# A hybrid decoder step on one core: score products over 128 rows, 1 - beta from ScalarE, and the mixer's stores on another queue

## The chip, the core and the metric

The kernel runs on one core of a Trainium2 chip. The core has TensorE (PE, matrix products; PEld is its weight load), VectorE (DVE), ScalarE (ACT), GpSimd (POOL), and SyncE (SP), which here only issues DMA. ACT can issue DMA too, on a queue of its own. Products are written to PSUM; everything else lives in SBUF or in DRAM. The metric is the time of one execution in microseconds, the median over runs.

## The reference

One inference step of two layers over 1024 prompt tokens and 8 samples of 8 new tokens each, width 1024, all in float32. Layer 0 is stick-breaking attention (16 heads of 64), layer 1 an RWKV-7 mixer (16 heads with a 64 x 64 state); each is followed by a squared-ReLU MLP of width 4096, and each of the four sub-layers has an adaptive RMS norm before it. For attention,

```
z = q.k / 8 + bias[head]
log_beta = log_sigmoid(z);  log_1mb = where(mask, log_beta - z, 0)     # log(1 - beta)
tail = reverse_cumsum(log_1mb) - log_1mb
a = where(mask, exp(log_beta + tail), 0);   o = a @ v
```

so each weight is beta times the product of (1 - beta) over all later keys. The prompt attends to itself; the samples attend to 2048 cached keys in pages of 128 and to their own. The mixer mixes each token with the one before it, makes r, k, v by dense products and the decay, rate and gate by low-rank ones, and runs a recurrence over the tokens:

```
S = S * w_t - (S @ kk_t) b_t^T + v_t k_t^T;   y_t = S @ r_t
```

## The kernel before

**Foreground and background.** The tokens go in two halves: A has 576 prompt tokens, B has 448 prompt tokens and the 64 sample tokens. Tiles have 128 features as rows and tokens as columns. Dense layers (`dense`, lines 328 to 341) are the foreground: each weight tile is split into a high part (`wh`, ACT, L321) and a low part (`wl`, POOL L323 and DVE L324), and each output tile takes three products for each of its feature tiles (L337 to L339) on 288 or 512 columns. After each such triple `step` is called; it advances generators: `self.work`, the background, by `rate` steps per 512 columns, and `self.side`, work that stands beside a stage. The background is attention of A, attention of B, attention of the samples, then for each half `rw_units` (the mixer's preparation) and `rw_chains` (the recurrence by chunks of 64 tokens). So the order in which Python traces instructions weaves both together. The tile framework then orders each engine's instructions by a simulated time line of its own (`schedule_with_timeline_sim=True`); on the chip each engine runs its list in that order.

**Stages.** qkv of A, qkv of B with attention A behind it, output projection and MLP of A with attention B and the samples behind them, `mixer_in` of A, output projection and MLP of B with the mixer of A behind them, `mixer_in` of B, then the rest.

**Scores.** `att_stacks` loads q, k and v of a pair of heads and makes for each head `qh`, the high part of q in both halves of the 128 rows, `kk`, the high part of k in its own 64 rows and the low part in the others, and `ql`, the low part of q in 64 rows. `att_prompt` makes a score tile z of 128 queries by up to 512 keys with two products: L552, `qh` against `kk` over 128 rows, and L554, `ql` against `kk` over 64 rows. Tiles of 64 queries take both heads at once with plain products (L550). `stick` turns z into weights: beta by a sigmoid on ACT (L509), a mask on POOL on the diagonal (L560, L562), 1 - beta on POOL (L512), the carry into the last column (L514, L516), a running product from the right on DVE (L518), and the weights (L519). The weights are transposed on PE (L126), copied by ACT (L576) and multiplied with v (L585). The samples use the same `stick` with tiles of 256 keys.

**Mixer.** `mixer_in` runs three dense products through `dense_to`, which copies each output tile out of PSUM, half the time by ACT and half by DVE (`copy`), and stores it (L963). Beside them stand `lora_rates` and `lora_gate`, which load the normed input again (L889) and mix it (`xmix`: ACT L814, DVE L817) for small products; `xsplit`, the same for the next dense product; and `rw_gate`, which loads a weight (L944, L945), multiplies and stores (L952). `rw_value` transposes v and stores it for the chunks (L981). In the background `rw_unit` prepares two heads: it loads k and r, runs a chain over all engines, and stores seven kinds of pieces (L1070, L1090, L1119, L1120, L1133 to L1135). After every three (A) or four (B) units `rw_lanes` inverts their 32 x 32 blocks by 31 steps of forward substitution on DVE (L1161, L1163), two steps of it for every step of a unit. All these loads and stores are issued by SP, in one list with the weight loads (L318), which ACT issues only while the samples are attended to.

Of the kernel before, what the change touches and what calls it, by code (L numbers as in the profile page):

```python
# [20 lines left out]
NT = 8  # L21
# [34 lines left out]
SLOT = 576  # L56
# [3 lines left out]
C_H16, C_SELN, C_MQ = 1056, 1072, 1200  # L60
C_N = 1264


def make_consts():
# [22 lines left out]
    c[:, C_MQ:C_MQ + 64] = t < s  # L87
    c[p % 32 == 0, C_SELN:C_SELN + 64] = 1.0
# [4 lines left out]
class Kern:  # L93
# [361 lines left out]
    def att_setup(self, lp):  # L455
# [9 lines left out]
        for hd, r in enumerate(self.R2):  # L465
            nc.vector.tensor_copy(self.bias_2[r, :], self.bias[r, hd::2])
        self.pt = lp.tile([1, 8 * PAGES], I32, name="pt")
# [6 lines left out]
    def att_stacks(self, m, pt, sp):  # L474

# [13 lines left out]
        ql = sp.tile([128, SLOT], F32R, tag="ql", name="ql")[:, :pt.NP]  # L489
        for hd in range(2):  # L490
# [10 lines left out]
        return q, k, qs, ql, ks, v  # L501

    def stick(self, z, w, bias, bp, tag, carry, mask):
# [4 lines left out]
        p = bp.tile([128, W + 1], F32, tag=tag + "p", name="prod", bufs=4 if tag == "p" else 3)  # L508
        nc.scalar.activation(beta[:, :w], z, AF.Sigmoid, bias=bias, scale=0.125)  # L509
        if mask:  # L510
            mask(beta)
        nc.gpsimd.tensor_scalar(p[:, :w], beta[:, :w], -1.0, 1.0, ALU.mult, ALU.add)  # L512
# [9 lines left out]
    def att_prompt(self, m, pt, sp, bp, ps):  # L522

        nc = self.nc
        q, k, qs, ql, ks, v = self.att_stacks(m, pt, sp)
# [7 lines left out]
        for c, end in sorted(tiles, key=lambda t: t[1] - t[0]):  # L533
# [7 lines left out]
            for j, (e0, e1) in enumerate(pieces):  # L541
# [3 lines left out]
                for x, hs in enumerate(heads):  # L545
                    z = ps.tile([128, 512], F32, tag="z", name="z")
                    for hd in hs:
                        a = self.R2[hd]
                        if both:
                            nc.tensor.matmul(z[a, :w], q[a, qc], k[a, e0:e1], start=True, stop=True)  # L550
                            continue
                        nc.tensor.matmul(z[:, :w], qs[hd][:, qc], ks[hd][:, e0:e1], start=True,  # L552
                                         stop=False)
                        nc.tensor.matmul(z[:, :w], ql[a, qc], ks[hd][a, e0:e1], start=False,  # L554
                                         stop=True)

                    def mask(beta, w=w):
                        d = beta[:, w - n:w]
                        if both:
                            nc.gpsimd.tensor_mul(d, d, self.cst[:, C_MQ:C_MQ + 64])  # L560
                        else:
                            nc.gpsimd.affine_select(out=d, in_=d, compare_op=ALU.is_gt, fill=0.0,  # L562
                                                    base=0, pattern=[[-1, 128]],
                                                    channel_multiplier=1)
                    bias = self.bias_2[:, m:m + 1] if both else \
                        self.bias[:, 2 * m + x:2 * m + x + 1]
                    al, carry[x] = self.stick(z[:, :w], w, bias, bp, "p", carry[x],
# [47 lines left out]
    def att_sample(self, sp, bp, ps):  # L615
# [38 lines left out]
        def new_keys(b, qbd):  # L654
# [7 lines left out]
            def mask(beta):  # L662
                nc.gpsimd.tensor_mul(beta[:, :8], beta[:, :8], self.cst[:, C_MN:C_MN + 8])
            al, carry = self.stick(z[:, :8], 8, self.bias_s, bp, "s", None, mask)
# [18 lines left out]
        for n, (b, j) in enumerate(steps):  # L683
# [6 lines left out]
            al, carry = self.stick(z[:, :256], 256, self.bias_s, bp, "s", carry, None)  # L690
# [194 lines left out]
    def lora_mixed(self, ns, f, pt, c0, n, tmp):  # L885
# [846 lines left out]
```

## Time and profile before

| | us |
|---|---|
| median of three runs (lowest, highest) | 3774.43 (3769.27, 3775.43) |
| the profiled execution: time, span | 3787.43, 3785.7 |
| PE, DVE, ACT, POOL busy in the span | 3562.3, 2331.9, 1467.7, 1351.5 |
| mean granted clock of TensorE | 0.959 |

The profile is that of one execution. A row of a group gives line, engine, operation, output and inputs by the program's names, shapes and count, then busy time in us and the mean duration of one in ns, then the engine's idle time just ahead of these instructions and what ended it. A row of waits names the waiting instruction, what it waited for, us in total, times, and the longest in us. In a list in order of time the first column is the start in us and the second the duration. Ends of products are modelled, so durations of neighbours overlap and the distance between starts says what a product costs. "SPq" and "ACTq" are the sequencers that issue DMA.

### The profile page before, as it was taken

To read this page: it belongs to the slowest core of one execution; us is meant where nothing else is said; L and a number is where in the kernel's file an instruction comes from. 1 tells how busy PE (TensorE), PEld (TensorE's weight loads), DVE (VectorE), ACT (ScalarE), POOL (GpSimd) and SP (SyncE) were. 2 spreads that over 40 slices of the span, in tenths; PEclk is the share of its full clock that TensorE was granted. 3 is DMA by queue.
4 is the path that set the end of the run, shared out by engine and by line. 5 is a ranking of instruction groups with operands and counts; after the bars stand their busy time and mean duration, and the time that the engine had idled before them with its cause. 6 is when DMAs were issued, how large, how long until landed. Compare 5 with 4: busy or idle time off the path is not lost.

```text
span 3785.7 us, 71776 instructions
## 1 busy us (share of the span) xinstructions
PE 3562.3 (94%) x26360; PEld 2806.3 (74%) x26360; DVE 2331.9 (62%) x4691; ACT 1467.7 (39%) x3042; POOL 1351.5 (36%) x1844
## 2 busy tenths in 40 slices
PE   8999999999999998996799999898989999989998
PEld 5886666678788885766577777565888888877887
DVE  4246768897555556677755556776885666645444
ACT  3133434444222234543334444563334334333332
POOL 1135546565322222323423333432222222343432
PEclk9999999999999998988889999899999999999999
DMA  8845434122888885566444344567634454333332
GB/s 307 279 141 177 145 108 128 50 75 71 315 326 311 334 325 209 185 202 183 130 124 147 116 136 129 167 212 220 196 88 135 131 147 138 111 106 100 101 93 84
DMA packets 431858, 632.37 MB, mean 167 GB/s; under 512 B 144210, under 2 KB 244435, under 8 KB 431507
## 3 DMA queue, kind: packets, MB, share of 16 engines
q1 hardware_dynamic: 417394, 593.17, 48.8%
q10 hardware_dynamic: 14112, 34.61, 2.6%
q8 instruction: 209, 3.42, 0.4%
q14 instruction: 143, 1.16, 0.1%
HBM read 521.62 MB, written 106.01 MB: 166 GB/s over the span
## 4 chain that ended last, share of the span: by engine, by line
PE 47%; DVE 7%; DMA 3%; issue 2%; ACT 1%; SPq 1%; POOL 1%; DVEq 0%; ACTq 0%; POOLq 0%
PE dq L337 12%; PE dq L338 12%; PE dq L339 12%; PE qc L1281 1%; DVE tm L1161 1%; PE s L1098 1%; PE qc L1271 1%; PE qc L1290 1%; DVE lxn L1163 1%; PE invq L1231 0%; PE bonq L1430 0%; PE yq L1438 0%; DMA x<-s_xn 0%; PE qc L1285 0%; PE invq L1240 0%
## 5 line engine op out<-in xcount | busy, mean ns | idle before, releaser
L323 POOL TENSOR_TENSOR wl<-wst,wh 128x256 fp32r<-128x256 f32 (+1 forms) x512 | 663.6, 1297 | 1497.8 <-ACT wh L321 1353.7
L337 PE MATMUL dq<-hhi,wh 128*128 128x288 f32 (+1 forms) x2112 | 712.8, 338 | 26.8 <-ACT hhi L118 26.1
L321 ACT CAST wh<-wst 128x512 fp32r<-128x512 f32 (+1 forms) x512 | 425.1, 834 | 793.0 <-PE dq L338 626.6
L338 PE MATMUL dq<-hlo,wh 128*128 128x288 f32 (+1 forms) x2112 | 706.7, 335 | 6.8 <-POOL hlo L290 4.3
L339 PE MATMUL dq<-hhi,wl 128*128 128x288 f32 (+1 forms) x2112 | 706.3, 335 | 0.5 <-POOL wl L323 0.5
L324 DVE TENSOR_TENSOR wl<-wst,wh 128x256 fp32r<-128x256 f32 (+1 forms) x512 | 365.1, 715 | 284.0 <-ACT wh L321 270.2
L338 PE MATMUL dq<-ul,wh 128*128 128x288 f32 (+1 forms) x1536 | 510.4, 333 | 0.0
L337 PE MATMUL dq<-uh,wh 128*128 128x288 f32 (+1 forms) x1536 | 508.7, 335 | 1.4 <-ACT wh L321 0.3
L339 PE MATMUL dq<-uh,wl 128*128 128x288 f32 (+1 forms) x1536 | 508.8, 333 | 0.0
L337 PEld LDWEIGHTS dq<-hhi,wh 128*128 128x128 f32 x2112 | 401.7, 191 | 78.0 <-ACT hhi L118 27.0
L338 PEld LDWEIGHTS dq<-hlo,wh 128*128 128x128 f32 x2112 | 401.5, 190 | 48.9 <-issue 10.9
L339 PEld LDWEIGHTS dq<-hhi,wl 128*128 128x128 f32 x2112 | 401.1, 190 | 45.5 <-issue 15.4
L352 DVE SCALAR_TENSOR_TENSOR x<-dq,mod,x 128x288 f32<-128x288 f32 (+1 forms) x432 | 245.5, 569 | 277.7 <-PE dq L339 275.4
L518 DVE TENSOR_TENSOR_SCAN prod<-prod 128x256 f32<-128x256 f32 (+5 forms) x264 | 253.0, 962 | 123.5 <-POOL prod L512 66.8
L337 PEld LDWEIGHTS dq<-uh,wh 128*128 128x128 f32 x1536 | 288.7, 188 | 42.3 <-issue 13.0
L339 PEld LDWEIGHTS dq<-uh,wl 128*128 128x128 f32 x1536 | 289.0, 188 | 34.7 <-issue 11.8
L338 PEld LDWEIGHTS dq<-ul,wh 128*128 128x128 f32 x1536 | 289.3, 188 | 29.0 <-issue 7.2
L512 POOL TENSOR_SCALAR prod<-beta 128x256 f32<-128x256 f32 (+5 forms) x264 | 170.9, 649 | 193.1 <-ACT beta L509 172.8
L337 PE MATMUL dq<-xhi,wh 128*128 128x288 f32 (+1 forms) x576 | 208.9, 363 | 11.4 <-DVE dn L120 7.2
L338 PE MATMUL dq<-xlo,wh 128*128 128x288 f32 (+1 forms) x576 | 202.5, 352 | 6.3 <-DVE xlo L290 4.0
L339 PE MATMUL dq<-xhi,wl 128*128 128x288 f32 (+1 forms) x576 | 200.4, 348 | 0.0
L445 DVE TENSOR_TENSOR ut<-ut 128x288 f32<-128x288 f32 (+1 forms) x192 | 163.4, 852 | 53.0 <-ACT ut L444 49.9
(290 smaller groups left out, 6191.7 us busy)
## 6 DMA issues: line engine op xcount, KB each, us to landing
pagek<-cache_kT SPq DMA_DIRECT2D x128, 512.0 KB
pagev<-cache_v SPq DMA_DIRECT2D x128, 512.0 KB
adaw<-ada_w SPq DMA_DIRECT2D x192, 256.0 KB
wst<-w_up SPq DMA_DIRECT2D x96, 512.0 KB
wst<-w_down SPq DMA_DIRECT2D x192, 256.0 KB
st<-s_st SPq DMA_DIRECT2D x40, 672.0 KB
wst<-sb_w_qkv SPq DMA_DIRECT2D x48, 512.0 KB
wst<-w_up ACTq DMA_DIRECT2D x32, 512.0 KB
```

What stands on the lines that cost most here:

```text
L321: nc.scalar.copy(wh, st)
L323: nc.gpsimd.tensor_sub(wl[:, :h], st[:, :h], wh[:, :h].bitcast(F32))
L324: nc.vector.tensor_sub(wl[:, h:], st[:, h:], wh[:, h:].bitcast(F32))
L337: nc.tensor.matmul(q, wh[:, k, :], h, start=k == 0, stop=False)
L338: nc.tensor.matmul(q, wh[:, k, :], l, start=False, stop=False)
L339: nc.tensor.matmul(q, wl[:, k, :], h, start=False, stop=k == kt - 1)
L352: nc.vector.scalar_tensor_tensor(xs, q[:, :np_], g, xs, ALU.mult, ALU.add)
L445: nc.vector.tensor_mul(t[:, :n], t[:, :n], t[:, :n])
L512: nc.gpsimd.tensor_scalar(p[:, :w], beta[:, :w], -1.0, 1.0, ALU.mult, ALU.add)
L518: nc.vector.tensor_tensor_scan(r, r, r, 1.0 if carry is None else carry, ALU.mult, ALU.bypass)
L1098: nc.tensor.matmul(qs[hd][:, 128 * x:128 * x + 128], BK[rows, u + x, 64 * hd:64 * hd + 128], AR[rows, :, c], start=True, stop=True)
L1161: eng.tensor_mul(t, lt[P, s, s + 1:32].unsqueeze(2).to_broadcast([N, a, c]), xn[P, s, 0:c].unsqueeze(1).to_broadcast([N, a, c]))
```

## The change

The low part of q is kept for each head in a tile of its own and copied by ACT into the other 64 rows too, so that L554's product also runs over 128 rows. It thereby adds the product of the two low parts. 1 - beta comes from a second sigmoid on ACT, of -z, written straight into the tile that the scan runs over, and the mask is applied to both tiles. In the mixer the stores of `dense_to`, `rw_gate`, `rw_value` and `rw_unit` go to ACT's queue (qkv's stay on SP's). `load_split`, the low-rank products and `rw_gate` load one tile ahead. `rw_lanes` waits eight steps after its loads and advances one step for every step of a unit.

```diff
     def load_split(self, src, pt, pool, tmp, parts):
-        for f in range(NT):
+        def load(f):
             t = tmp.tile([128, pt.W], F32, tag="n", name="t")
             self.nc.sync.dma_start(t, src[f][:, pt.cols])
+            return t
+        ahead = load(0)
+        for f in range(NT):
+            t, ahead = ahead, load(f + 1) if f + 1 < NT else None
...
     def att_stacks(self, m, pt, sp):
...
-        ql = sp.tile([128, SLOT], F32R, tag="ql", name="ql")[:, :pt.NP]
         for hd in range(2):
...
+            ql = sp.tile([128, SLOT], F32R, tag=f"ql{hd}", name="ql")[:, :pt.NP]
             nc.gpsimd.tensor_sub(ql[a], q[a], qh[a].bitcast(F32))
-            qs.append(qh)
+            nc.scalar.copy(ql[b], ql[a].bitcast(F32))
+            qs.append((qh, ql))
...
-    def stick(self, z, w, bias, bp, tag, carry, mask):
+    def stick(self, z, w, bias, nbias, bp, tag, carry, mask):
...
+        nc.scalar.activation(p[:, :w], z, AF.Sigmoid, bias=nbias, scale=-0.125)
         nc.scalar.activation(beta[:, :w], z, AF.Sigmoid, bias=bias, scale=0.125)
         if mask:
-            mask(beta)
-        nc.gpsimd.tensor_scalar(p[:, :w], beta[:, :w], -1.0, 1.0, ALU.mult, ALU.add)
+            mask(p, beta)
         if carry is None:
             nc.gpsimd.memset(p[:, w:w + 1], 1.0)
         else:
-            nc.gpsimd.tensor_scalar(p[:, w:w + 1], carry, 1.0, 0.0, ALU.mult, ALU.add)
+            nc.gpsimd.tensor_copy(p[:, w:w + 1], carry)
...
-                        nc.tensor.matmul(z[:, :w], qs[hd][:, qc], ks[hd][:, e0:e1], start=True,
-                                         stop=False)
-                        nc.tensor.matmul(z[:, :w], ql[a, qc], ks[hd][a, e0:e1], start=False,
-                                         stop=True)
+                        for i, part in enumerate(qs[hd]):
+                            nc.tensor.matmul(z[:, :w], part[:, qc], ks[hd][:, e0:e1], start=i == 0,
+                                             stop=i == 1)
-                    def mask(beta, w=w):
...
+                    def mask(p, beta, w=w):
+                        for t, fill in ((p, 1.0), (beta, 0.0)):
+                            d = t[:, w - n:w]
+                            if both and t is p:
+                                nc.vector.tensor_max(d, d, self.cst[:, C_MQ1:C_MQ1 + 64])
+                            elif both:
+                                nc.gpsimd.tensor_mul(d, d, self.cst[:, C_MQ:C_MQ + 64])
+                            else:
+                                nc.gpsimd.affine_select(out=d, in_=d, compare_op=ALU.is_gt,
+                                                        fill=fill, base=0, pattern=[[-1, 128]],
+                                                        channel_multiplier=1)
...
+            def mask(p, beta):
+                nc.vector.tensor_max(p[:, :8], p[:, :8], self.cst[:, C_MN1:C_MN1 + 8])
...
+    def lora_loads(self, pt, c0, n, tmp):
...
+        for f in range(NT):
+            h = tmp.tile([128, SLOT], F32, tag="n", name="hc")
+            self.nc.sync.dma_start(h[:, :n + e], self.hscr[f][:, pt.o + c0 - e:pt.o + c0 + n])
+            tiles.append(h)
+            if f:
+                yield tiles[f - 1]
+        yield tiles[-1]
...
-            for f in range(NT):
+            for f, h in enumerate(self.lora_loads(pt, c0, n, tmp)):
...
     def rw_gate(self, pt, tmp, ps):
-        for m in range(NT):
+        def load(m):
...
+        ahead = load(0)
+        yield
+        for m in range(NT):
+            (ga, gb), ahead = ahead, load(m + 1) if m + 1 < NT else None
...
-            nc.sync.dma_start(self.s_g[m][:, pt.cols], t)
+            nc.scalar.dma_start(self.s_g[m][:, pt.cols], t)
...
-    def dense_to(self, w, hi, lo, pt, tmp, ps, dst, then=None):
+    def dense_to(self, w, hi, lo, pt, tmp, ps, dst, then=None, queue=None):
...
-                self.nc.sync.dma_start(dst[m][:, pt.cols], t)
+                (queue or self.nc.sync).dma_start(dst[m][:, pt.cols], t)
...
-                    nc.sync.dma_start(self.s_v[m, hd][:, c + p:c + p + 2 * nw - 1:2, :],
+                    nc.scalar.dma_start(self.s_v[m, hd][:, c + p:c + p + 2 * nw - 1:2, :],
...
-        nc.sync.dma_start(self.s_p[m][:, pt.cols], t1[:, :W])
+        nc.scalar.dma_start(self.s_p[m][:, pt.cols], t1[:, :W])
...
-            nc.sync.dma_start(sst[self.R2[hd], hd, :], AR[self.R2[hd], 0, :W])
+            nc.scalar.dma_start(sst[self.R2[hd], hd, :], AR[self.R2[hd], 0, :W])
...
     def rw_lanes(self, ms, pt, pool):
...
-        yield
+        for _ in range(8):
+            yield
...
                 for _ in self.rw_unit(m, i, pp, ps):
                     next(lanes, None)
-                    next(lanes, None)
                     yield
...
-        self.dense_to(I["rw_w_r"], *r, pt, tmp, PS, self.s_r)
+        self.dense_to(I["rw_w_r"], *r, pt, tmp, PS, self.s_r, None, self.nc.scalar)
```

The other four store lines of `rw_unit` (two for S, one for AR, one for L, as L1119, L1120 and L1133 to L1135 were) and the other two dense products of `mixer_in` change in the same way. The negated biases are made once, and the constants grow by 72 columns for the two masks that set 1.

More of the change, by code (lines that the diff above doesn't have):

```diff
@@ L59 @@
 C_ID, C_SEL9, C_SELB, C_MN, C_M64, C_M8, C_BLK, C_B8 = 0, 128, 144, 656, 664, 792, 920, 1048
-C_H16, C_SELN, C_MQ = 1056, 1072, 1200
-C_N = 1264
+C_H16, C_SELN, C_MQ, C_MQ1, C_MN1 = 1056, 1072, 1200, 1264, 1328
+C_N = 1336
 def make_consts():
@@ L87, in make_consts @@
     c[:, C_MQ:C_MQ + 64] = t < s
+    c[:, C_MQ1:C_MQ1 + 64] = t >= s
+    c[:, C_MN1:C_MN1 + 8] = 1.0 - c[:, C_MN:C_MN + 8]
     c[p % 32 == 0, C_SELN:C_SELN + 64] = 1.0
@@ L466, in att_setup @@
             nc.vector.tensor_copy(self.bias_2[r, :], self.bias[r, hd::2])
+        for name, t in (("nbias", self.bias), ("nbias_s", self.bias_s), ("nbias_2", self.bias_2)):
+            setattr(self, name, lp.tile(list(t.shape), F32, name=name))
+            nc.vector.tensor_scalar(getattr(self, name), t, -1.0, None, ALU.mult)
         self.pt = lp.tile([1, 8 * PAGES], I32, name="pt")
@@ L524, in att_prompt @@
         nc = self.nc
-        q, k, qs, ql, ks, v = self.att_stacks(m, pt, sp)
+        q, k, qs, ks, v = self.att_stacks(m, pt, sp)
         yield
@@ L551, in att_prompt @@
                             continue
-                        nc.tensor.matmul(z[:, :w], qs[hd][:, qc], ks[hd][:, e0:e1], start=True,
-                                         stop=False)
-                        nc.tensor.matmul(z[:, :w], ql[a, qc], ks[hd][a, e0:e1], start=False,
-                                         stop=True)
-                    def mask(beta, w=w):
[L558 to L567, printed above, removed]
+                        for i, part in enumerate(qs[hd]):
[12 more added lines that the diff above has]
+                                                        channel_multiplier=1)
+                    bias, nbias = (t[:, m:m + 1] for t in (self.bias_2, self.nbias_2)) if both else \
+                        (t[:, 2 * m + x:2 * m + x + 1] for t in (self.bias, self.nbias))
+                    al, carry[x] = self.stick(z[:, :w], w, bias, nbias, bp, "p", carry[x],
                                               None if j else mask)
@@ L660, in new_keys @@
                                      ks[:, m, 8 * b:8 * b + 8], start=p == 0, stop=p == 1)
-            def mask(beta):
+            def mask(p, beta):
+                nc.vector.tensor_max(p[:, :8], p[:, :8], self.cst[:, C_MN1:C_MN1 + 8])
                 nc.gpsimd.tensor_mul(beta[:, :8], beta[:, :8], self.cst[:, C_MN:C_MN + 8])
-            al, carry = self.stick(z[:, :8], 8, self.bias_s, bp, "s", None, mask)
+            al, carry = self.stick(z[:, :8], 8, self.bias_s, self.nbias_s, bp, "s", None, mask)
             a64 = bp.tile([128, 64], F32, tag="a64", name="a64")
@@ L689, in att_sample @@
                 yield
-            al, carry = self.stick(z[:, :256], 256, self.bias_s, bp, "s", carry, None)
+            al, carry = self.stick(z[:, :256], 256, self.bias_s, self.nbias_s, bp, "s", carry, None)
             yield
@@ L883, in rw_shift, with lora_mixed @@
         self.nc.sync.dma_start(self.O["shiftT"], self.last[:, :, 0:9])
-    def lora_mixed(self, ns, f, pt, c0, n, tmp):
+    def lora_loads(self, pt, c0, n, tmp):
         e = 1 if pt.o + c0 else 0
-        h = tmp.tile([128, SLOT], F32, tag="n", name="hc")
-        self.nc.sync.dma_start(h[:, :n + e], self.hscr[f][:, pt.o + c0 - e:pt.o + c0 + n])
+        tiles = []
+        for f in range(NT):
[5 more added lines that the diff above has]
+        yield tiles[-1]
+    def lora_mixed(self, ns, f, h, pt, c0, n, tmp):
+        e = 1 if pt.o + c0 else 0
         out = []
@@ L925, in lora_gate @@
             nb = [(u * n // 4, (u + 1) * n // 4) for u in range(4)]
-            for f in range(NT):
+            for f, h in enumerate(self.lora_loads(pt, c0, n, tmp)):
                 st = dict(start=f == 0, stop=f == NT - 1)
-                xg, = self.lora_mixed((5,), f, pt, c0, n, tmp)
+                xg, = self.lora_mixed((5,), f, h, pt, c0, n, tmp)
                 nc.tensor.matmul(qg[:, :n], ga[:, f, :], xg, **st)
@@ L1118, in rw_unit @@
             orow = self.R2[1 - hd]
-            nc.sync.dma_start(sst[orow, hd, :], S[0][orow, :W])
-            nc.sync.dma_start(sst[:, 2 + hd, :], S[1 + hd][:, :W])
+            nc.scalar.dma_start(sst[orow, hd, :], S[0][orow, :W])
+            nc.scalar.dma_start(sst[:, 2 + hd, :], S[1 + hd][:, :W])
         for u in range(0, nch, 5):
@@ L1132, in rw_unit @@
         for hd in range(2):
-            nc.sync.dma_start(sst[:, 4 + hd, :], S[3 + hd][:, :W])
-        nc.sync.dma_start(sst[:, 6, :], AR[:, 1, :W])
-        nc.sync.dma_start(self.s_l[m][:, c0:c0 + nch, :], L[:, :W].rearrange("p (c t) -> p c t", c=nch))
+            nc.scalar.dma_start(sst[:, 4 + hd, :], S[3 + hd][:, :W])
+        nc.scalar.dma_start(sst[:, 6, :], AR[:, 1, :W])
+        nc.scalar.dma_start(self.s_l[m][:, c0:c0 + nch, :], L[:, :W].rearrange("p (c t) -> p c t", c=nch))
         yield
@@ L1624, in mixer_in @@
         self.dense_to(I["rw_w_k"], *k, pt, tmp, PS, self.s_k,
-                      lambda m, t: self.ready.add(("k", i, m)))
+                      lambda m, t: self.ready.add(("k", i, m)), self.nc.scalar)
         def value(m, t):
```

7 lines of the change are left out of this document (4 added, 3 removed).

## The prediction

> **What bounds the kernel now.** I read the page first, then a table of stretches of the span, then single instructions of TensorE in order of time, and at last the groups and waits of the other engines.
>
> ```profile
> PE 3562.3 (94%) x26360; PEld 2806.3 (74%) x26360; DVE 2331.9 (62%) x4691; ACT 1467.7 (39%) x3042; POOL 1351.5 (36%) x1844
> ```
>
> TensorE (PE) is busy for 94% of the span, and no other engine for more than 62%. So work taken from PE's own queue counts first; work on other engines counts only where PE waits for it. An average over stages says little, so here are the stages (prompt attention of the first half, of the second half, attention of the samples, the mixer of the first half, a feed-forward stage, the mixer of the second half). The columns are the stretch, its length, busy time of the five engines, granted clock, DMA share, GB/s.
>
> ```profile
> 210.00:600.00 390.00, 372.74 (x2353) 267.69 (x2351) 264.31 (x378) 160.07 (x316) 210.87 (x357) 0.97 0.44 141
> 600.00:930.00 330.00, 319.40 (x2298) 245.34 (x2298) 278.48 (x364) 156.97 (x301) 185.87 (x279) 0.97 0.23 63
> 930.00:1430.00 500.00, 495.05 (x4805) 402.77 (x4803) 257.61 (x504) 146.19 (x294) 146.53 (x274) 1.00 0.87 322
> 1430.00:1890.00 460.00, 375.10 (x2492) 294.14 (x2485) 318.66 (x668) 202.59 (x382) 142.32 (x130) 0.86 0.57 178
> 1890.00:2370.00 480.00, 473.49 (x3499) 360.72 (x3498) 269.31 (x667) 200.73 (x509) 164.78 (x221) 0.98 0.45 132
> 2370.00:2790.00 420.00, 368.90 (x2340) 267.86 (x2338) 313.46 (x706) 202.71 (x383) 142.99 (x185) 0.91 0.60 185
> ```
>
> In prompt attention (210 to 930) PE is busy 692 of 720 us: PE's queue sets the pace. In the sample stage PE has 495 of 500 and the DMA engines 0.87. The mixers (1430 to 1890, 2370 to 2790) are different: PE idles 84.9 + 51.1 = 136 us at a granted clock of 0.86 and 0.91, and VectorE (DVE) is busy 632 of 880 us. There PE waits for others.
>
> Now the score products. L552 is the first product, L554 the second; the difference between starts is what each costs on PE.
>
> ```profile
> 764.34 0.50 PE L552 MATMUL z<-kk,qh 128*128 128x512 f32 x1
> 764.78 0.50 PE L554 MATMUL z<-kk,ql 64*128 64x512 f32 x1
> 765.21 0.40 PE L339 MATMUL dq<-hhi,wl 128*128 128x288 f32 x1
> 765.45 0.29 PE L337 MATMUL dq<-hhi,wh 128*128 128x288 f32 x1
> 765.58 0.29 PE L338 MATMUL dq<-hlo,wh 128*128 128x288 f32 x1
> ...
> 768.69 0.40 PE L552 MATMUL z<-kk,qh 128*128 128x512 f32 x1
> 769.01 0.50 PE L554 MATMUL z<-kk,ql 64*128 64x512 f32 x1
> 769.44 0.55 PE L126 MATMUL tq<-cst,beta 128*128 128x128 f32 x3
> ```
>
> And 512 columns in an unbroken run of 128-row products, from the last feed-forward stage:
>
> ```profile
> 3550.00 0.39 PE L337 MATMUL dq<-hhi,wh 128*128 128x512 f32 x1
> 3550.23 0.39 PE L338 MATMUL dq<-hlo,wh 128*128 128x512 f32 x1
> ```
>
> Steady, 512 columns cost 0.23 us. Around a 64-row product they do not: at 768.69 the 128-row product holds PE 0.32 us before the 64-row one starts (+0.09), the 64-row one holds it 0.43 (+0.20), and the first 128-row product after one (765.21) holds it 0.24 where the next takes 0.13 (+0.11). Half the rows save nothing, and each change of row count costs at both edges.
>
> **The change part by part.**
>
> *Score passes.* The second product gets 128 rows. Its number of columns and of instructions stays:
>
> ```profile
> L554 PE MATMUL z<-kk,ql x160: 322/467/793, 220.5 to 918.6; 64*128 64x512 f32 x80, 64*128 64x256 f32 x32, 64*128 64x384 f32 x32, 64*128 64x128 f32 x16
> ```
>
> Per pair 0.09 + 0.20 + 0.11 = 0.40 us go if 128-row products stand on both sides, 0.29 if something of another shape follows (it then pays the edge anyway). 160 pairs: 46 to 64 us of PE time; most pairs stand in a dense stream, so I take 0.38, 61 us. By the loops 64 pairs belong to the first half (24 us) and 96 to the second (37 us).
>
> How much of that reaches the end? In 210 to 600 DVE and ScalarE (ACT) have room (264 and 160 of 390): I take 80%, 19 us. In 600 to 930 PE would need 330 - 37 = 293 us of stretch, and DVE has 278 us of work there: 95%. I take 70%, 26 us. Together 45 us; the ends are 61 (all of it) and 0 (another engine takes over at once).
>
> *The second sigmoid* costs ACT one more pass for each score tile, plus two copies of the low part for each head pair, priced by the copy of the same shape (L495):
>
> ```profile
> L509 ACT ACTIVATE beta<-z,bias 128x512 f32<-128x512 f32 (+4 forms) x192 | 111.7, 584 | 34.7 <-PE z L554 18.2 <-issue 8.2 <-PE tq L126 3.5
> ...
> L509 ACT ACTIVATE beta<-zs,bias_s 128x256 f32<-128x256 f32 x64 | 30.3, 474 | 80.0 <-PE zs L649 67.6 <-DVE a L667 5.1 <-PE dq L339 3.8
> ...
> L495 ACT CAST qh<-q 64x576 fp32r<-64x576 f32 (+1 forms) x32 | 19.8, 618 | 10.1 <-PE z L552 5.8 <-POOL wl L323 2.7 <-DMA q<-s_q 1.0
> ```
>
> That is 111.7 + 30.3 + 19.8 = 162 us. In 600 to 930 it is 112 of the 192 prompt tiles (65 us) and half of the copies (10): ACT goes from 157 to 232 of about 300 us. Cover: ACT's own idle time. If the cover fails, what is late next is the copy of the transposed scores (L576) and the weight cast (L321), which stand behind on the same engine, and then PE. The score tile in PSUM, of which there are two, is held one sigmoid longer. In the sample stage 30 us on an ACT with 146 of 500 busy lie under DMA and PE: 0.
>
> GpSimd (POOL) loses its pass and gains one more mask for each diagonal tile:
>
> ```profile
> L512 POOL TENSOR_SCALAR prod<-beta 128x256 f32<-128x256 f32 (+5 forms) x264 | 170.9, 649 | 193.1 <-ACT beta L509 172.8 <-PE dq L339 10.0 <-PE o L585 0.3
> L562 POOL TENSOR_SCALAR_AFFINE_SELECT beta<-beta 128x128 f32<-128x128 f32 x112 | 55.0, 494 | 107.3 <-ACT beta L509 105.3 <-PE adaq L212 1.1
> ```
>
> Net 170.9 - 55.0 = 116 us less on POOL, off PE's path: 0 by itself, and the chain from score to scan is one pass of 0.65 us shorter. The 24 small maxima on DVE, the carry copy and the wider constants I cost at 0: they lie under PE's stream, and without that cover the maxima are some 24 x 0.5 = 12 us by the mask's row.
>
> *Stores on ACT's queue.* 320 issues leave SyncE's queue (SP) and enter ACT's, in the mixers alone: 48 of the dense results, 80 of the values, 96 of the first S and AR pieces, 96 others. The columns are shortest, median and longest issue in ns.
>
> ```profile
> L963 SPq DMA_DIRECT2D s_k<-dn x16: 319/320/523, 1548.2 to 2563.4; - x16
> ...
> L981 SPq DMA_DIRECT2D s_v<-vt x80: 452/610/1473, 1668.3 to 2680.2; - x80
> ...
> L1120 SPq DMA_DIRECT2D s_st<-S x32: 397/536/601, 1576.5 to 2778.1; - x32
> ```
>
> 48 x 0.32 + 80 x 0.61 + 192 x 0.536 = 167 us, the last term high for the "others". ACT is busy 405 of 880 us there, so 572 with them. Each store also carries its wait:
>
> ```profile
> SPq L963 <- DVE dn L120: 116.1, 40, 11.0
> ...
> SPq L1119 <- DVE L L1112: 30.9, 11, 14.3
> ```
>
> A part of the first (which holds the attention's stores too) and the second now stop ACT in order; behind them stand weight casts, PSUM copies and the mixing activations, for which PE waits. What SP gains: loads no longer queue behind stores.
>
> [...]
>
> *Loads one tile ahead* go at this wait, which sits on ACT in both mixers:
>
> ```profile
> ACT xw L814 <- DMA hc<-hscr: 60.4, 26, 6.7
> ```
>
> At best 60 us of ACT time, on the path only where a low-rank product waits for it. *Block inverses spread*: one step of them per unit step instead of two, and eight empty steps after their loads. The work stays:
>
> ```profile
> L1161 DVE TENSOR_TENSOR tm<-llt,lxn 108x31 f32<-108x31 f32 (+23 forms) x80 | 35.8, 447 | 8.8 <-DMA llt<-s_l 7.5
> L1163 DVE TENSOR_TENSOR lxn<-lxn,tm 108x31 f32<-108x31 f32 (+23 forms) x80 | 34.3, 429 | 1.3
> ```
>
> 70 us of DVE in the first mixer (1470 to 1890), now in smaller doses between copies that PE waits for; the 7.5 us of waiting for their load goes. The last batch has no unit beside it and ends 8 steps later.
>
> Mixer term: the best is half of PE's 136 idle us, -68; the worst is the 167 us plus waits with a quarter to a half of it reaching PE, +80. The row nearest to the truth is PE's idle time, of which ACT's load wait is a cause and ACT's new issues a new one; I take -10.
>
> *Sum* against the profiled execution's own 3787.4 us (span 3785.7): -45 - 10 = -55, so 3732. The three timed runs have their median 13.0 us below that execution, so 3774.4 - 55 = **3719 us**.
>
> **The rivals.**
> 1. *All of it arrives and the mixers clear up*: -61 and -50, 3663 us. For: PE is the bound in attention, and the mixers idle 136 us. Against: DVE at 95%.
> 2. *Another engine takes the attention gain*: DVE, and ACT at 232 of 300, leave 12 of 45 us; mixers 0. 3762 us. It includes that the planner, which orders the instructions by its own simulated times, sets the two products apart from each other or moves waits by as much as is won.
> 3. *Slower: stores block ACT.* Place: ACT's queue in the mixers. Price: 167 us of issues and up to 116 + 31 us of waits. It decides when more than 45 us of these 314 reach PE; at 80 the result is -45 + 80, 3809 us. For: DVE at 632 of 880 us is late with just the copies for which the stores wait. Against: the planner places a store where it believes the data ready, and weights are cast up to three tiles ahead. [...]
>
> **How the numbers follow.** The forecast (3695 to 3745 its own range) has 0.48, rival 1 0.14, rival 2 0.20, rival 3 0.18. This kernel's runs tell a change from none at about 0.2%, 7.5 us: 3767 to 3782 is "the same". Of rival 2 some 0.08 falls there and of rival 3 0.03, so faster 0.74, same 0.11, slower 0.15. The range holds rival 1 and the forecast and most of rival 2: 3655 to 3782.
>
> **What would show it.** Right: the second product's row says 128 rows, follows the first after 0.23 us, and the product after it takes its steady time; prompt attention takes some 675 us instead of 720; ACT's busy time in it rises by about 130 us and POOL's falls by 100; in the mixers the waits for hc vanish. Rival 2: prompt attention keeps 700 us or more, with PE waiting for DVE or ACT. Rival 3: the mixers grow beyond 880 us in sum, with waits of ACT's sequencer for DVE's copies ahead of weight casts. Wrong altogether: a change of order that puts new PE waits into stages the diff doesn't touch.

## The result and the profile after

The changed kernel takes 3717.82 us (median of four, 3712.77 to 3723.21) beside 3774.93 us for the kernel before on the same chip: ratio 0.9846, 95% interval 0.9826 to 0.9865. The forecast was 3719. The profiled execution's span fell from 3785.7 to 3710.8 us, which is 18 us more than the medians differ: the profiled execution before is 12.5 us above its median and the one after 5 us below. First the page's line of busy time, after:

```profile
PE 3497.1 (94%) x26360; PEld 2785.7 (75%) x26360; DVE 2320.9 (63%) x4718; ACT 1594.7 (43%) x3342; POOL 1235.3 (33%) x1692
```

TensorE (PE) has the same 26360 products and 65 us less busy time; ScalarE (ACT) has 127 us more, GpSimd (POOL) 116 less. PE is still the bound.

**Prompt attention.** The score products in order of time, after (start, duration):

```profile
759.83 0.39 PE L564 MATMUL z<-kk,qh 128*128 128x512 f32 x1
760.06 0.40 PE L564 MATMUL z<-kk,ql 128*128 128x512 f32 x1
760.29 0.29 PE L341 MATMUL dq<-hhi,wl 128*128 128x288 f32 x1
760.42 0.29 PE L339 MATMUL dq<-hhi,wh 128*128 128x288 f32 x1
```

In this pair all three edges are gone: 0.23 us from the first product to the second, 0.23 to the dense one, and 0.13 to the next. Over all pairs of 512 columns in the two traces the medians go from 0.40 to 0.31 us from the first product to the second, from 0.43 to 0.24 to the one behind, and from 0.24 to 0.13 behind that where it is dense: together 0.39 us less. The 0.31 isn't the steady 0.23 because most first products that follow a transpose still take 0.31 to 0.32 (behind a dense product the median is 0.23); that edge did not come from the row count.

Two stretches follow, from the first prompt score to the first sample score and from there to the first mixer, with the columns of the prediction's table; first before:

```profile
211.70:947.30 735.60, 707.69 (x4782) 527.98 (x4781) 548.36 (x753) 318.68 (x620) 402.31 (x651) 0.97 0.35 109
947.30:1436.40 489.10, 479.76 (x4681) 386.94 (x4681) 257.38 (x500) 150.43 (x301) 143.35 (x262) 0.99 0.87 325
```

and after:

```profile
214.30:891.80 677.50, 642.51 (x4715) 511.52 (x4717) 529.19 (x767) 420.09 (x843) 320.01 (x571) 0.97 0.38 117
891.80:1390.70 498.90, 491.05 (x4772) 397.77 (x4771) 255.99 (x512) 176.00 (x372) 127.53 (x194) 0.99 0.88 327
```

The first stretch is 58 us shorter and the second 10 longer: 67 fewer products stand in the first and 91 more in the second, since the scores end while the dense layer beside them is less far on. Over both, PE's busy time falls by 1187.45 - 1133.56 = 54 us and the length by 48; the first score starts 2.6 us later, so the mixer starts 45.7 us earlier. PE's idle time in them, length less busy time, rises from 37 to 43 us.

**From the first mixer to the end.** Five stretches: first mixer with the output projection after it, MLP of B, second mixer with its projection, the last MLP of A, and the sum from the first mixer to the end. Before:

```profile
1436.40:1888.30 451.90, 371.46 (x2456) 292.23 (x2456) 312.04 (x659) 194.79 (x367) 138.22 (x119) 0.86 0.57 175
1888.30:2404.70 516.40, 500.42 (x3790) 381.35 (x3790) 294.94 (x732) 226.08 (x575) 184.57 (x267) 0.96 0.46 137
2404.70:2766.10 361.40, 321.19 (x1891) 227.61 (x1889) 269.55 (x597) 168.11 (x300) 122.37 (x144) 0.92 0.61 188
2766.10:3342.90 576.80, 571.84 (x5140) 502.98 (x5140) 372.90 (x915) 223.49 (x596) 160.40 (x171) 1.00 0.44 129
1436.40:3785.70 2349.30, 2176.41 (x15216) 1739.38 (x15216) 1456.99 (x3268) 949.86 (x2051) 769.94 (x905) 0.94 0.47 142
```

After:

```profile
1390.70:1813.50 422.80, 361.48 (x2442) 283.46 (x2438) 309.12 (x628) 193.76 (x368) 131.31 (x115) 0.90 0.58 181
1813.50:2297.70 484.20, 475.23 (x3451) 359.44 (x3451) 284.03 (x691) 205.50 (x508) 175.48 (x260) 0.97 0.45 135
2297.70:2663.10 365.40, 326.55 (x2095) 232.60 (x2093) 261.42 (x585) 172.58 (x337) 116.89 (x137) 0.92 0.58 182
2663.10:3268.30 605.20, 590.77 (x5276) 513.51 (x5276) 402.76 (x997) 239.30 (x631) 165.38 (x185) 0.99 0.46 134
1390.70:3710.80 2320.10, 2165.41 (x15202) 1723.95 (x15198) 1464.59 (x3266) 948.65 (x2056) 753.22 (x901) 0.95 0.47 142
```

Length less PE busy is PE's idle time. It falls from 80.4 to 61.3 us in the first mixer and from 16.0 to 9.0 in the MLP beside its chains, and rises from 5.0 to 14.4 in the last MLP of A, which now carries 136 products more. The sum is 29 us shorter: 18 us less idle (172.9 to 154.7) and 11 us less busy time for nearly the same products, at a granted clock of 0.95 instead of 0.94. The idle time is the firmer of the two: a second execution of the changed kernel (`after_again` below) has 156.8 us of it and 13 us less busy time, and `nudge_before`, which runs the kernel before in the same order, has 80.7 us of idle time in a first mixer that is 9 us shorter (443.1 us at a clock of 0.89). So 10 us in a stage's length can belong to the execution.

**The waits that the edits aimed at.** Two groups of ACT after (the second sigmoid; the mixing of the low-rank inputs):

```profile
L520 ACT ACTIVATE prod<-z,nbias 128x512 f32<-128x512 f32 (+4 forms) x192 | 113.0, 589 | 53.5 <-PE z L564 25.2 <-DVE prod L529 9.0 <-PE z L561 5.9
...
L828 ACT ACTIVATE xw<-hc,omm 128x288 f32<-128x288 f32 (+1 forms) x72 | 41.0, 593 | 37.2 <-DVE xw L831 12.6 <-PE loq L933 11.9 <-DMA hc<-hscr 6.0
```

The wait for hc fell from 60.4 to 6.0 us. ACT's own queue, the stores of the dense results and of the values after (shortest, median and longest in ns; the second view ends with who waited for that line):

```profile
L992 ACTq EVENT_SEMAPHORE  x30: 17/17/5262, 1413.8 to 2565.1; - x30
L992 ACTq DMA_DIRECT2D s_k<-dn x16: 325/326/514, 1495.9 to 2459.4; - x16
...
L1010 ACTq DMA_DIRECT2D s_v<-vt x80: 463/622/1280, 1599.9 to 2574.8; - x80
who waited for it (us, times):
  ACT wh L323: 7.6, 1
  ACT shi L120: 4.6, 1
```

The issues cost on ACT what they cost on SP (medians of 0.33 us for s_k and 0.62 for s_v, 0.32 and 0.61 on SP before), and the median wait ahead of a store is 17 ns, on the nine other store lines too: the data were ready, but for six of these 189 waits, of 5.3, 4.7, 3.9, 3.5, 1.0 and 0.5 us. Rival 3 did not happen.

### The profile page after: what moved, and what is told of

It reads as the page before. It is cut to its first block, busy times and chain, and to the rows that moved or that the text cites. A ratio compares the mean times of both kernels' runs of the same rounds, so it can differ in the third digit from the quotient of the medians.

```text
span 3710.8 us, 72191 instructions
## 1 busy us (share of the span) xinstructions
PE 3497.1 (94%) x26360; PEld 2785.7 (75%) x26360; DVE 2320.9 (63%) x4718; ACT 1594.7 (43%) x3342; POOL 1235.3 (33%) x1692
## 4 chain that ended last, share of the span: by engine, by line
PE 40%; DVE 7%; DMA 3%; issue 2%; POOL 1%; ACT 1%; SPq 1%; ACTq 0%; DVEq 0%; POOLq 0%
PE dq L339 11%; PE dq L340 11%; PE dq L341 10%; DVE lxn L1193 1%; DVE tm L1191 1%; PE qc L1310 1%; PE qc L1300 1%; PE qc L1319 1%; PE yq L1467 1%; PE bonq L1459 0%; PE qc L1314 0%; PE invq L1260 0%; DMA s_v<-vt 0%; DVE wl L326 0%; PE qc L1323 0%
## 5 line engine op out<-in xcount | busy, mean ns | idle before, releaser
L325 POOL TENSOR_TENSOR wl<-wst,wh 128x256 fp32r<-128x256 f32 (+1 forms) x512 | 648.0, 1267 | 1580.3 <-ACT wh L323 1367.6
L326 DVE TENSOR_TENSOR wl<-wst,wh 128x256 fp32r<-128x256 f32 (+1 forms) x512 | 353.8, 694 | 264.6 <-ACT wh L323 226.2
L451 DVE TENSOR_TENSOR ut<-ut 128x288 f32<-128x288 f32 (+1 forms) x192 | 153.1, 798 | 40.5 <-ACT ut L450 37.8
L453 ACT CAST uh<-ut 128x288 fp32r<-128x288 f32 (+1 forms) x192 | 95.2, 496 | 189.2 <-DVE ut L451 186.8
```

The costliest lines, as they stand in the source:

```text
L325: nc.gpsimd.tensor_sub(wl[:, :h], st[:, :h], wh[:, :h].bitcast(F32))
L326: nc.vector.tensor_sub(wl[:, h:], st[:, h:], wh[:, h:].bitcast(F32))
L451: nc.vector.tensor_mul(t[:, :n], t[:, :n], t[:, :n])
L453: nc.scalar.copy(a, t[:, :n])
```

## The experiments

Times are medians; the ratio is to the kernel before, run on the same chip, with its 95% interval. "Start" is where the first mixer begins, "rest" from there to the end of the profiled execution, "idle" the part of the rest in which PE isn't busy, all in us. The rows of stretches such as those above carry them.

| kernel | parts of the change in it | time | ratio | start | rest | idle |
|---|---|---|---|---|---|---|
| before | none | 3774.9 | | 1436.4 | 2349.3 | 172.9 |
| `nudge_before` | none | 3777.2 | 1.0003 [0.9989, 1.0018] | 1432.0 | 2343.9 | 171.8 |
| `sigmoid_only` | second sigmoid | 3773.0 | 0.9991 [0.9981, 1.0001] | 1431.1 | 2344.0 | 170.5 |
| `rows_only` | 128 rows | 3735.2 | 0.9895 [0.9878, 0.9913] | 1400.4 | 2333.7 | 169.7 |
| `attn_only` | 128 rows, second sigmoid | 3741.7 | 0.9907 [0.9891, 0.9923] | 1390.0 | 2352.4 | 173.4 |
| `mixer_only` | the mixer's three edits | 3776.7 | 1.0007 [0.9998, 1.0015] | 1426.8 | 2342.3 | 167.0 |
| `rows_mixer` | 128 rows, mixer | 3762.2 | 0.9963 [0.9950, 0.9975] | 1397.3 | 2367.9 | 182.9 |
| `no_stores` | all but the stores' queue | 3725.5 | 0.9864 [0.9848, 0.9881] | 1394.5 | 2325.2 | 168.1 |
| `no_ahead` | all but the loads ahead | 3739.6 | 0.9904 [0.9888, 0.9921] | 1391.0 | 2352.5 | 168.3 |
| `no_lanes` | all but the spread inverses | 3750.0 | 0.9930 [0.9914, 0.9946] | 1389.8 | 2358.2 | 176.8 |
| after | all | 3717.8 | 0.9846 [0.9826, 0.9865] | 1390.7 | 2320.1 | 154.7 |
| `after_again` | all | 3707.9 | 0.9817 [0.9801, 0.9833] | 1389.9 | 2309.4 | 156.8 |
| `nudge_after` | all | 3711.7 | 0.9831 [0.9811, 0.9852] | 1390.9 | 2318.8 | 154.7 |
| `steps9` | all, one empty step more | 3709.4 | 0.9828 [0.9808, 0.9847] | 1390.8 | 2310.1 | 155.2 |

**The halves of the change.** `attn_only` is the kernel before with the hunks of `att_stacks`, `att_prompt` and `stick`; `mixer_only` has the other hunks.

```diff
-                        nc.tensor.matmul(z[:, :w], ql[a, qc], ks[hd][a, e0:e1], start=False,
-                                         stop=True)
+                        for i, part in enumerate(qs[hd]):
+                            nc.tensor.matmul(z[:, :w], part[:, qc], ks[hd][:, e0:e1], start=i == 0,
+                                             stop=i == 1)
```

> The kernel before with the attention's part of the change alone: second score product over 128 rows, 1 - beta as a second sigmoid, masks on both tiles. The mixer is as before. Own theory (PE time given back by the row count, some of it eaten by DVE and ACT): 45 us less than before, 0.988 of it, and the stages up to the start of the first mixer end about 45 us earlier while the later ones keep their lengths. Rival (another engine takes the gain): at most 12 us less, 0.997 or more.

> The kernel before with the mixer's part alone: stores on ACT's queue, loads one tile ahead, block inverses spread. Attention is as before. Own theory: 10 us less than before, 0.997. Rival 1 (the mixers clear up): 30 us or more less, 0.992 or below. Rival 3 (stores block ACT): the same or slower, 1.000 or above, with waits of ACT for DVE's copies in the mixers.

Attention alone is worth 34 us in the run times, not the 45 expected. The mixer's three edits alone are worth nothing that can be measured. That is the time that rival 3 named, but without its sign: the two mixers have 808 us instead of 813, and ACT's waits behind the issue of the values are six single cases of 1.8 to 5.1 us. Yet on top of attention the same edits bring 23 to 34 us (0.9907 to 0.9846 and 0.9817). The rest of `mixer_only`, in the stretches used above:

```profile
1426.80:1857.50 430.70, 365.17 (x2457) 285.36 (x2457) 310.10 (x634) 194.19 (x367) 133.98 (x119) 0.89 0.59 184
1857.50:2355.70 498.20, 482.77 (x3529) 368.73 (x3529) 289.63 (x718) 212.17 (x527) 181.66 (x269) 0.97 0.45 135
2355.70:2733.30 377.60, 333.71 (x2084) 238.32 (x2082) 267.94 (x598) 174.04 (x333) 114.86 (x136) 0.88 0.59 183
2733.30:3325.80 592.50, 581.42 (x5208) 507.85 (x5208) 387.42 (x953) 234.14 (x614) 165.80 (x177) 0.98 0.44 130
```

Its first mixer and the MLP beside the chains are 39 us shorter than before (-21 and -18), and its second mixer and last MLP of A 32 longer (+16 and +16): what the edits win early is handed back late. Part of both is work that moved, since the MLP beside the chains has 261 products fewer and the two later stages 261 more. In PE's idle time the four differences are -15, -1, +4 and +6. In the changed kernel the lengths differ by -29, -32, +4 and +28.

**The halves of the attention part.** `rows_only` keeps 1 - beta on GpSimd; `sigmoid_only` keeps the second product at 64 rows. From the edit of `sigmoid_only`:

```diff
+        nc.scalar.activation(p[:, :w], z, AF.Sigmoid, bias=nbias, scale=-0.125)
...
-        nc.gpsimd.tensor_scalar(p[:, :w], beta[:, :w], -1.0, 1.0, ALU.mult, ALU.add)
```

> Of the attention's part only the row count: the low part of q copied by ACT into the other 64 rows, the second product over 128 rows; 1 - beta stays on POOL. Own theory: the row count carries the gain, 35 to 45 us less than before (0.988 to 0.991), the second product starts 0.23 us after the first. Rival: the gain needs the second sigmoid too (POOL and DVE in the way), 20 us or less.

> Of the attention's part only the second sigmoid and its masks; the second product stays over 64 rows. Own theory: PE is the bound and gets no time back, so within 8 us of before (0.998 to 1.002), although POOL loses about 116 us and ACT gains about 144. Rival (the chain from score to weights or DVE's contention with POOL sets the pace): 15 us or more less.

The row count carries the gain. The second sigmoid alone is within the noise; on top of the row count the mixer starts some 8 us earlier with it (1397.3 and 1400.4 against 1389.8 to 1394.5). The run times of the two kernels without the mixer's edits don't show that: 3735.2 us without it, 3741.7 with it. The hold between VectorE and GpSimd that the rival of `sigmoid_only` names does show in the trace before: of the weights' 96 multiplications on 128x512 (L519) the 27 with GpSimd idle take VectorE at most 0.69 us, the 52 with GpSimd busy for more than 60% of their time 0.87 on average and 1.92 at most. But it did not set the pace: `sigmoid_only` takes 3773.0 us.

What the second sigmoid does on top of the row count can be seen from the first prompt score to the first mixer. The sum of the two stretches in `rows_only`, and PE's waits there:

```profile
sum 1189.80, PE 1136.72 PEld 908.98 DVE 801.71 ACT 484.17 POOL 561.12; mean PE 568.36 PEld 454.49 DVE 400.85 ACT 242.08 POOL 280.56
```

```profile
PE tq L126 <- DVE beta L520: 20.6, 19, 4.2
...
PE o L585 <- DMA v<-v_prompt: 6.9, 2, 3.9
PE dq L338 <- POOL hlo L290: 5.4, 1, 5.4
```

The wait for VectorE's weights (the first row) was 4.8 us before, and in the changed kernel it is

```profile
PE tq L128 <- DVE beta L530: 19.5, 13, 5.4
```

With the row count alone PE's busy time falls by 51 us for as many products (9465 after 9463), which is 0.32 us a pair, and the length by 35 (1224.7 to 1189.8). PE idles 53 us there, 37 before and 43 in the changed kernel. Other traces repeat this: `rows_mixer` has 52, and the kernels with the whole attention part have 40 to 44. So VectorE takes some 15 us of the gain either way. With the row count alone other waits grow too, for a load of v and for GpSimd's splits, and the second sigmoid takes 116 us of work off GpSimd. About 70% of the gain becomes length without it and 90% with it (35 of 51, 48 of 54). Which of the small waits decides was not followed.

**One mixer edit left out.** `no_stores` puts the 320 stores back on SP, `no_ahead` loads again where the tile is used, `no_lanes` goes back to one empty step and two steps for each step of a unit. `after_again` is the changed kernel itself, run beside them. One place of each edit, in this order:

```diff
-            nc.scalar.dma_start(sst[orow, hd, :], S[0][orow, :W])
+            nc.sync.dma_start(sst[orow, hd, :], S[0][orow, :W])
...
-            for f, h in enumerate(self.lora_loads(pt, c0, n, tmp)):
+            for f in range(NT):
...
-        for _ in range(8):
-            yield
+        yield
```

> The changed kernel once more, beside the three kernels that each leave one mixer edit out. Expected 0.9846 of before again (57 us less). Its trace is a second profile of the same program: where two profiles of one kernel differ by stage, smaller differences between kernels say nothing.

> The changed kernel with all the mixer's stores back on SP's queue; loads ahead and spread inverses stay. Theory S (the stores are what makes the mixer's part worth 23 us on top of the attention's): about 23 us slower than the changed kernel, 0.991 of before. Theory L (the loads ahead do it): the same as the changed kernel, 0.985. Theory P (the planner's order, which every edit moves): somewhere within 25 us of the changed kernel without a pattern over the three.

> The changed kernel with the loads of the low-rank products, the gate and the split tiles where they were, not one tile ahead. Theory S: the same as the changed kernel, 0.985. Theory L: about 23 us slower, 0.991, with ACT's wait for hc back at about 60 us. Theory P: no pattern.

> The changed kernel with the block inverses as before (two steps of them for each step of a unit, one empty step after their loads). Own theory: 0 to 10 us slower, since DVE's copies wait behind denser inverse steps in the first mixer, or 0 to 10 us faster, since the second mixer's background ends sooner; the stage table tells which. Theory P: no pattern.

Against `after_again`, leaving out one edit costs 18 (stores), 32 (loads ahead) and 42 us (inverses). Leaving out all three costs 34 by the same comparison, so these are no shares that add up. Neither theory S (the stores carry the gain) nor theory L (the loads ahead do) fits all three, although in `no_ahead` ACT's wait for hc is back, at 48.3 us; theory P's 25 us are exceeded twice, and the 0 to 10 us expected for the inverses were far too few. What the stores do locally can still be read. The first mixer of `no_stores`, and its sum:

```profile
1394.50:1839.50 445.00, 363.38 (x2442) 288.22 (x2438) 319.33 (x667) 194.94 (x368) 135.37 (x115) 0.86 0.56 172
...
1394.50:3719.70 2325.20, 2157.14 (x15202) 1723.51 (x15198) 1464.83 (x3266) 951.94 (x2054) 760.16 (x901) 0.95 0.47 142
```

PE idles 81.6 us in that mixer, 61.3 with the stores on ACT's queue. Over all the traces there is no overlap: the six with the mixer's stores on SP have 74.6 to 82.4 us (before 80.4), the eight with them on ACT 61.2 to 71.2 (`mixer_only` 65.5). The waits of SP and of PE in this mixer of `no_stores`:

```profile
PE vq L128 <- DVE dn L122: 14.2, 3, 10.7
...
SPq L991 <- DVE dn L122: 34.7, 14, 11.1
SPq L1147 <- DVE S L1137: 28.3, 8, 7.4
SPq L1118 <- DVE AR L1103: 17.9, 7, 5.6
SPq L1162 <- POOL AR L1104: 12.8, 3, 5.3
```

and of the changed kernel, in the same order:

```profile
PE vq L128 <- DVE dn L122: 2.2, 1, 2.2
...
SPq L320 <- DVE wl L326: 106.2, 25, 26.2
SPq L1182 <- DMA s_l<-L: 35.4, 5, 13.1
```

On SP the stores in these four rows held the queue for 94 us until their data came; without them SP runs ahead to the weight loads and waits there for a free buffer (106.2 us, 31.9 in `no_stores`). So the store move takes 11 to 20 us of PE's idle time out of the first mixer: 20 in this pair, 11, 13 and 15 where all three edits are added to `rows_only`, to `attn_only` and to the kernel before. PE's row for v (vq) is 12 of the 20; its other rows go both ways, and how the waits on SP lead to the rest was not followed. But `no_stores` has 582.2 us in its last MLP of A, 23 less than the changed kernel, and ends 18 us behind `after_again` in the run times. (That MLP has 136 products fewer in `no_stores`.) Leaving out the inverses' spreading shows mostly in the second mixer, here of `no_lanes`: 51.7 us idle (385.90 - 334.22) instead of 38.9.

```profile
2309.60:2695.50 385.90, 334.22 (x2047) 237.09 (x2045) 262.76 (x586) 172.82 (x332) 116.27 (x136) 0.89 0.58 176
```

**Chance of the order, or a mechanism that needs all three?** The last four runs were to tell this.

```diff
-        nc = self.nc
+        nc = self.nc; nc.vector.memset(lp.tile([128, 1], F32, name="nudge"), 0.0)
...
-        for _ in range(8):
+        for _ in range(9):
```

> The changed kernel with one memset of 128 x 1 more on VectorE ahead of the mixers; no work, wait or transfer of weight is changed, but the instructions are ordered anew from the first mixer on. Theory P (the 23 to 34 us of the mixer edits on top of the attention edits come from the order that the planner happens to find): 3715 to 3745 us, 10 to 25 us away from the changed kernel, lost as often as not in the mixers. Rival theory M (the three edits need each other by a mechanism, so every order has their gain): within 6 us of the changed kernel, ratio to before 0.981 to 0.985.

> The kernel before with the same memset. Theory P: 5 to 25 us away from the kernel before, to either side (ratio outside 0.999 to 1.001). Theory M: within 4 us (0.999 to 1.001), since the order is not what counts.

> The changed kernel with nine empty steps after the loads of the inverses instead of eight: a smaller disturbance of the order than the memset. Theory P: 3 to 20 us away from the changed kernel. Theory M: within 4 us of it, 0.981 to 0.985 of before.

> The changed kernel without the second sigmoid: 128 rows in the second score product and the whole mixer part, 1 - beta again from GpSimd. Prompt attention 10 us longer than in the changed kernel (36 us of the 46 won). Theory M: the mixer edits keep their gain on top, so 3720 to 3728 us. Theory P: the order is drawn again, 3712 to 3750 us, with the gain behind attention anywhere between 0 and 40 us.

The first three stay within 4 us of `after_again` and of the kernel before, which reads like theory M, but they were no test. Set side by side in order of start, the instructions of `nudge_after` and `steps9` from the first mixer on are those of the changed kernel in the same order on all engines (all but a handful of PE's 15,197, where a few records are missing), and `nudge_before` keeps that of the kernel before. The memset and the ninth step disturbed nothing; the expectation was wrong that they would. What these runs show is that one order repeats its time: 3707.9, 3709.4, 3711.7 and, in the first comparison, 3717.8 us.

`rows_mixer` was a real test and both theories missed it: 3762 us, by the ratios 26 us slower than `rows_only`, though it only adds the three mixer edits. Theory M falls with it, since all three edits are in. Its sum, and that of `rows_only`:

```profile
1397.30:3765.20 2367.90, 2184.97 (x15216) 1743.75 (x15216) 1466.67 (x3268) 951.82 (x2055) 761.05 (x905) 0.94 0.47 140
```

```profile
1400.40:3734.10 2333.70, 2164.05 (x15216) 1725.28 (x15216) 1459.30 (x3268) 949.27 (x2051) 764.41 (x905) 0.95 0.47 143
```

13 us more idle and 21 us more busy time for the same 15,216 products, at a clock of 0.94 instead of 0.95. So the same three edits gain nothing on the kernel before, lose 26 us on the row count alone and gain 23 to 34 us on the whole attention part. Between kernels whose mixer code is the same the order does differ: of PE's 15,216 products from the first mixer on, 13,019 stand in a common order in the kernel before and `attn_only`, and 11,650 in `rows_mixer` and the changed kernel. Counted in the same way, the orders fall into groups. `mixer_only`, `rows_mixer` and `no_lanes` have 13,583 to 13,735 products in common with one another, though `no_lanes` lacks the spread inverses and the other two have them; beside the same attention without the mixer's edits they gain 0 and lose 26 and 9 us. The kernels without any of the mixer's edits form another group with `no_stores` and `no_ahead`; those two gain 16 and 1 us. The changed kernel has at most 12,047 in common with any kernel of another order, and it alone gains 23 to 34. The gain thus goes with the order at least as much as with the list of edits. That the order decides is therefore likely, not shown: no run changed the order and nothing else.

## Why the prediction was right or wrong

**What bounds it** was right: PE's queue in prompt attention, waits in the mixers.

**Row count.** The mechanism and the price were right. 0.38 us for each of 160 pairs was forecast as 61 us of PE time; 54 us came with the whole change, 0.34 a pair, and 51 with the row count alone. The medians show the three edges falling by what was read from single pairs. Mis-sized is how many pairs have the third edge: 0.38 takes it for some 130 of the 160, but in the trace before a dense product stands behind 92. By the medians, 160 x 0.28 + 92 x 0.11 would have been 55 us.

**How much arrives.** 19 + 26 = 45 us were forecast; the mixer starts 45.7 us earlier. This is luck: misses that cancel. The shares of 80% and 70% were near for the row count alone, where 35 of 51 us became length; they were too low for the whole change, where 48 of 54 did. VectorE did hold PE back, by some 15 us of added waits in both; what the prediction had at nothing is that the second sigmoid takes other waits away. PE's smaller gain and a later first score went the other way. Over several executions it is less: kernels with the attention of before start the mixer at 1426.8 to 1436.4 (mean 1431.7), those with the whole of the new one at 1389.8 to 1394.5 (mean 1391.0), so the term is -41. Prompt attention itself shrank more than the 45 us named as its sign, and the sample stage, costed at 0, gave 10 back, because dense work moved into it.

**The second sigmoid** was costed at 0 on the path: `sigmoid_only` agrees, and the 8 us on top of the row count were not foreseen, although the prediction had named the chain from score to scan that it shortens. GpSimd's 116 us came as 116, ACT's 162 as 127, in part since the two sigmoids of one tile overlap: their durations add up to 294.6 us and cover 265.4. In prompt attention alone ACT rose by 101 us (130 named as the sign) and GpSimd fell by 82 (100 named). After, on the sample scores (shortest, median, longest in ns, first and last start in us):

```profile
L520 ACT ACTIVATE prod<-zs,nbias_s x64: 467/475/503, 892.9 to 1396.6; 128x256 f32<-128x256 f32 x64
L521 ACT ACTIVATE beta<-zs,bias_s x64: 463/468/487, 893.3 to 1396.9; 128x256 f32<-128x256 f32 x64
```

Each lasts 0.47 us, and the second starts 0.3 to 0.4 us after the first.

**The mixer term** was -10, with bounds of -68 and +80. On top of the attention part it was -23 to -34, 13 to 24 us larger than taken. Its steps: the waits for hc went as said (60.4 to 6.0), and SP's loads no longer queue behind stores, which takes 11 to 20 us of PE idle time from the first mixer. The step that failed is the pricing itself: the term was treated as one number that belongs to the edits. Alone the edits bring 0, on the row count alone they lose. The value -10 was right for neither; it lay between cases that I didn't tell apart. The prediction named a change of order in stages the diff doesn't touch as what would prove it wrong; `attn_only` and `rows_only` have the same mixer code and differ by 19 us behind attention (2352.4, 2333.7). Two executions of the changed kernel differ by 11 there, and PE's idle time differs by 4 (173.4, 169.7), so this is a weak sign of it. The hit of 3719 within 2 us is luck: attention alone brought 34 us in the run times where 45 were forecast, and the mixer term, a size that no row carried, made up for it.

**The store move.** `mixer_only`, with the two other edits in it, took 1.0007 of the time of the kernel before, no gain in the total; `no_stores` ended 18 us behind `after_again`. In the first mixer the measurement goes further: what the move took from SP were 94 us of waits in order, while an issue cost about the same on either queue, and PE's idle time fell from 81.6 to 61.3 us.

**Rivals.** Rival 1 needed idle time of PE to fall by 50 us; it fell by 18. Rival 2 needed prompt attention at 700 us or more with PE waiting for another engine; it is 678 from first score to first sample score. With the row count alone it is 699, with 20.6 us of waits for VectorE's weights: there its sign is nearly met, and the kernel gains 36 us up to the first mixer all the same. Rival 3 needed more time in the two mixers, with ACT waiting for copies; their stretches went from 813 to 788 us, and the stores' median wait is 17 ns. Its price was partly there: ACT waited behind the issue of the values in four single cases of 4 to 8 us, and started nothing during three of the waits ahead of a dense result's store (5.3, 4.7 and 3.5 us).

**The sum.** In run times attention is -34 (the -41 at the mixer's start, less 6 lost behind it) and the mixer part -23 to -34, which makes -57 to -68; the four comparisons of the whole change give -57 to -69. The forecast of -55 lies at the near end.

## What to carry to other kernels

A product over half the rows saved no time here beside products over all of them, and cost 0.32 us a pair more: fill the rows where the added result is harmless. Work that is costed at 0 because another engine is the bound can still decide how much of that engine's gain becomes time: look at what the engine waits for once it is faster. When an order is made by a planner, price local gains locally (here the idle time of PE in one stage) and expect the total to keep only part of them; run an edit together with the others before judging it, because alone, on half of the change and on the whole it gave 0, a loss and a gain. Compare idle time of the bound engine before lengths, since two executions of one program can differ by 13 us in busy time. A "small disturbance" is a test of the order only if the order was seen to change.

## What the runs showed of the hardware that was not expected

A load that reads what another queue has stored can hold its own queue. SP's loads of the pieces for the inverses, before and then after, wait for the store that is now on ACT's queue:

```profile
SPq L1153 <- DMA s_l<-L: 9.6, 8, 2.0
```

```profile
SPq L1182 <- DMA s_l<-L: 59.0, 11, 13.1
```

With both on SP, the load seldom stood long at the head of the queue before its data had landed; with the store elsewhere SP arrives early and stands, 59.0 us in all. In the first mixer it is 35.4 us, and 5.9 in `no_stores`, with both on SP again. No run tells what that costs the end.

PE's busy time for the same products is not constant. Among the kernels with 15,202 products after the start of the first mixer it goes from 2152.6 us at a granted clock of 0.96 (`after_again`) to 2184.2 at 0.94 (`no_ahead`):

```profile
1389.90:3699.30 2309.40, 2152.63 (x15202) 1714.05 (x15198) 1463.45 (x3266) 951.24 (x2056) 753.56 (x901) 0.96 0.47 143
```

```profile
1391.00:3743.50 2352.50, 2184.22 (x15202) 1744.02 (x15198) 1458.61 (x3266) 948.36 (x2052) 752.04 (x901) 0.94 0.46 140
```

The first profile of the same program as `after_again` has 2165.4 at 0.95, with 2 us less idle time. Mostly the kernels with more idle time have the lower clock: 167.0 to 182.9 us idle at 0.94, 154.7 to 173.4 at 0.95, 155.2 and 156.8 at 0.96. But `no_stores` (168.1 idle, 2157.1 busy, 0.95) and `no_ahead` (168.3, 2184.2, 0.94) differ at the same idle time.
